# Coarser picks, later listing and a re-planned order in a two-layer PEER backbone

## The chip, the cores and the metric

One core of one Trainium2 chip runs the whole program. The metric is device microseconds of one execution. Engines are named as in the profile: PE (matrix products) with PEld (its weight loads), DVE (vector), ACT (scalar), POOL, and SP, which issues most loads.

## What is computed

The reference is a backbone of two layers over 256 tokens of width 1024. Layer 0 mixes state-space (SSD) and latent-attention heads (`hybrid`), layer 1 is a chunked gated MLP (`gmlp`). Each layer has modulation vectors (`cond @ ada_w`) and ends in a PEER block: each token picks, in each of 8 heads, its 16 best of 128 x 128 experts by two keys, and adds them, gated.

```python
q = (t @ wq).reshape(n_tok, PEER_HEADS, PEER_DKEY)
s1 = einsum('thd,hkd->thk', q[..., :half], k1); s2 = einsum('thd,hkd->thk', q[..., half:], k2)
v1, i1 = top_k(s1, 16); v2, i2 = top_k(s2, 16)
top_s, j = top_k(v1[..., :, None] + v2[..., None, :], 16)      # flattened 16 x 16
idx = 128 * i1 + i2 at j;  gate = softmax(top_s)
act = gelu(einsum('phkd,pd->phk', u_tab[idx], t))
out = einsum('phk,phkd->pd', gate * act, v_tab[idx])
```

## The kernel before

All engines run in-order queues. Their order is set while the program is built, by a planner: `Clock` keeps a modelled time for each engine, `Engine.cost` gives each instruction a price, and `schedule()` always takes the next step of whichever generator (a stream of work) is ready soonest. A `yield` of a condition, such as `at(tile)`, holds a stream back until the modelled clock says that the tile is there. So prices in `cost` move instructions, though they change nothing on the chip. Every recorded instruction goes through one wrapper, and thus stands at line L169 in the profile (L173 in the changed kernel).

**The modulation products** (`ada_group`) load 128 x 512 pieces of `ada_w` into a few buffers `aw` and multiply each by `condT` into 32 of 128 rows of a PSUM tile. They are strewn among the other products of `hybrid`, at the planner's choice.

**The PEER block** (`peer`) treats the experts by their first index, the class. The 75 classes 0 to X-1 are done densely: 75 S tiles (`products`, `pa<-phf,wr`) score 128 experts each for all 256 tokens, 75 V tiles (`pb<-wr,ge`) multiply the weighted scores by the value table. Tile data come through four buffers `wr`, loaded from SP's queue. Between them stands `spread`: 32 blocks of 8 tokens whose gates DVE writes out as one-hot tables (`o`, `oc`); PE multiplies these (`pb<-oc,o`), and DVE, or ACT where the score is not there yet, applies the result to `ge`. No V tile may begin before the last block is applied (the flag "G").

The experts of the other 53 classes are gathered. Each of two token tiles has CAP = 56 own rows: for row s, POOL fetches for each of 128 tokens one expert's u and v (2,048 floats, 1.05 MB a row) by an indirect DMA (`rows<-in_uv,gidx`), DVE takes the dot product (`junk`), ACT the GELU and gate, and DVE adds the weighted v (`acc`). Six row buffers (NR) are in use, and a row's `acc` comes two rows (LAG) after its dot. What does not fit into 56 goes to three shared rows: `listing` counts the leftovers of each token (`cnt`), sums them with small matrix products, builds `cmp` and `spot`, and PE adds the shared rows into the V sums (`pb<-rows,sc`).

Which experts a row holds comes from the picks. `choose` builds a key per expert and token, (row, place) packed into one float, and `take8` picks the 8 largest: one MAX8, one MATCH_REPLACE, small operations, and eight 128-wide `mk` operations that look up the gates. Nine picks per token tile are made, two of them ahead of the spread (EARLY), the rest one by one inside `gather`, between rows; only after the last does `listing` start. `ending` stores the sum of the first token tile (`acs`) and loads it again through SP's queue, in order with the tile loads.

Of the kernel before, what the change touches and what calls it, by code (L numbers as in the profile page):

```python
# [28 lines left out]
ROOM = 36  # L29
TB, TL = 8, 4  # L30
CAP = 56
ROUNDS = 9
# [18 lines left out]
KORDER = (8, 10, 12, 0, 2, 4, 6, 14)  # L51
LAG = 2
# [78 lines left out]
class Engine:  # L131
# [5 lines left out]
    def __getattr__(self, op):  # L137
        f = getattr(self.eng, op)

        def call(*args, **kw):  # L140
# [5 lines left out]
            if op == "indirect_dma_start":  # L146
# [3 lines left out]
                self.clock.run("D", 0.06 + 1.4e-3 * outs[0].shape[1], outs, ins, 2.0)  # L150
# [22 lines left out]
    def cost(self, op, outs, ins):  # L173
        aps = outs + ins
        if self.name == "T":
            n = 1
            for x in aps[-1 if op == "matmul" else 0].shape[1:]:
                n *= x
            return max(0.025, n * (0.00167 if aps[1].dtype == F32 else 0.00042)) * (0.25 if aps[0].shape[0] == 32 else 1.0)
        n = 1  # L180
        for x in aps:
            m = 1
            for y in x.shape[1:]:
                m *= y
            n = max(n, m)
        if self.name == "S":
            return (0.24 if len(ins) > 2 else 0.1) + 0.00083 * n
        if self.name == "G":
            return 0.1 + 0.00215 * n
        if all(x.dtype == F16 for x in aps):  # L190
            return 0.07 + n * 0.00052
        if op == "tensor_scalar":
            return 0.18 + n * 0.00105 if ins[0].tensor.name[:3] in ("pa_", "pb_") else 0.12 + n * 0.00054
        return (0.12 if op == "scalar_tensor_tensor" else 0.06) + n * 0.00105
# [3 lines left out]
def tile_backbone(ctx: ExitStack, tc: tile.TileContext, a: dict, out: bass.AP):  # L198
# [51 lines left out]
    def mm(o, lhsT, rhs, start=True, stop=True):  # L250
        T.matmul(o, lhsT, rhs, start=start, stop=stop)
# [50 lines left out]
    LEFT = 8 * ROUNDS - CAP  # L302
# [191 lines left out]
    def ada_group(l, g, get, bufs, ps):  # L494
# [3 lines left out]
        for i in range(len(units) + n - 1):  # L498
            if i < len(units):
                k, t = units[i]  # L500
                aw = bufs[i % n]
                yield lambda: clk["T"] >= clock.idle(aw)
                Q.dma_start(out=aw, in_=a["ada_w"][l, k * P:(k + 1) * P, g * 2048 + t * 512:g * 2048 + (t + 1) * 512])
            if i >= n - 1:
                k, t = units[i - n + 1]
                aw = bufs[(i - n + 1) % n]
                yield at(aw)
                mm(ps[32 * t:32 * t + 32, :], condT[:, k, :], aw, k == 0, k == KD - 1)
# [904 lines left out]
    def peer(l, mod, a2, sh2):  # L1413
# [4 lines left out]
        key = [[q1.tile([P, P], F32, name=f"key{t}{i}") for i in range(2)] for t in range(2)]  # L1418
        iota_i = key[0][0].bitcast(I32)
        G.iota(iota_i, [[1, P]], base=0, channel_multiplier=0)  # L1420
        jp1 = q1.tile([P, P], F32, name="jp1")
        V.tensor_scalar(jp1, iota_i, 1.0, None, op0=ALU.add)
# [16 lines left out]
        gidx = [q1.tile([P, 8 * ROUNDS], I32, name=f"gidx{t}") for t in range(2)]  # L1439
        gsel = [q1.tile([P, 8 * ROUNDS], F32, name=f"gsel{t}") for t in range(2)]  # L1440
# [48 lines left out]
        def stage2(t):  # L1489
# [94 lines left out]
            V.scalar_tensor_tensor(key[t][0], cg, 256.0, jp1, op0=ALU.mult, op1=ALU.add)  # L1584
            V.tensor_tensor(key[t][0], key[t][0], mk, op=ALU.mult)
            pks.append(pk)
# [3 lines left out]
        EARLY = 2  # L1590
# [7 lines left out]
        def take8(t, r_, idx=None, gsl=None):  # L1598

            if idx is None:  # L1600
                idx, gsl = gidx[t][:, 8 * r_:8 * r_ + 8], gsel[t][:, 8 * r_:8 * r_ + 8]
            ks = q2.tile([P, 8], F32, tag="ks", name="ks")
            V.max(ks, key[t][r_ % 2])
            V.match_replace(key[t][(r_ + 1) % 2], ks, key[t][r_ % 2], 0.0)
            ki = q2.tile([P, 8], I32, tag="ki", name="ki")
            V.tensor_copy(ki, ks)
            z_ = q2.tile([P, 8], F32, tag="z_", name="z_")
            V.tensor_scalar(z_, ks, 0.0, 65536.0, op0=ALU.is_equal, op1=ALU.mult)
            V.tensor_scalar(idx, ki, 8, None, op0=ALU.logical_shift_right)
            V.tensor_tensor(idx, idx, z_, op=ALU.add)  # L1610
            V.tensor_scalar(ki, ki, 255, None, op0=ALU.bitwise_and)
            j1 = q2.tile([P, 8], F32, tag="j1", name="j1")
            V.tensor_copy(j1, ki)
# [146 lines left out]
        def choose():  # L1760
# [8 lines left out]
            for r_ in range(EARLY):  # L1769
                take8(0, r_)  # L1770
# [38 lines left out]
        def listing():  # L1809

            ps = pa()
            rhs = q2.tile([P, 2, 2], F32, tag="rhs", name="rhs", bufs=1)
            V.memset(rhs, 1.0)
            for t in range(2):
# [9 lines left out]
                V.tensor_reduce(fl, key[t][ROUNDS % 2], axis=AX.X, op=ALU.max)  # L1824
                V.tensor_scalar(fl, fl, 0.0, None, op0=ALU.is_gt)
                mm(ps[:, t:t + 1], tri, cnt[:, t:t + 1], True, t == 0)
# [3 lines left out]
                mm(ps[:, 3 + 2 * t:4 + 2 * t], ones, fl)  # L1830
# [3 lines left out]
            V.tensor_tensor(ends[:, 2:4], ends[:, 2:4], ps[:, 4:6], op=ALU.add)  # L1834
            ps = pa()
            for k in range(SHARED):
                for t in range(2):
                    cmp = q2.tile([P, P], F32, tag="cmp", name="cmp", bufs=4)
                    V.tensor_scalar(cmp, iotaL[:, :P], float(k * P), ends[:, t:t + 1], op0=ALU.add, op1=ALU.is_ge)
# [291 lines left out]
```

## Time and profile before

| what | value |
| --- | --- |
| time, median of 3 runs | 2041.65 us (2041.55 to 2047.14) |
| the profiled execution | 2042.83 us, of which the span 2041.0 us |
| PE busy | 1886.9 us, 92% of the span |
| DVE busy | 1429.6 us, 70% |
| POOL, ACT busy | 630.8 us, 545.9 us |
| mean granted clock of PE | 0.961 |
| V products begin | 841.11 us (first layer), 1716.72 us (second) |

Busy time is an average over stages: PE is nearly always busy, so the time can only shrink where PE stands idle or where its own work shrinks. The idle places are read from the waits and from the timeline, stage by stage: the hybrid mix up to some 400 us, the stretch of scores and spread, the V products, and the end of each layer.

### The profile page before, as it was taken

What the parts mean: (1) busy time and instruction counts of PE and PEld (TensorE: products, weight loads), DVE (VectorE), ACT (ScalarE), POOL (GpSimd) and SP (SyncE); (2) the same over time, 40 slices, a digit from 0 to 9 for tenths busy, and PEclk for the clock granted to TensorE, in tenths of its full rate; (3) what the DMA queues carried; (4) which work ended last, traced back from release to release, by engine and by line L of the source; (5) the groups of instructions that cost most, each with busy time, mean ns of one, the idle gap of its engine ahead of it and who ended that gap; (6) DMA issues with size and microseconds to landing.
All of it is one profiled execution on the core that took longest, in us unless ns stands there. A gap on an engine that the chain in (4) does not pass through costs nothing.

```text
span 2041.0 us, 28033 instructions
## 1 busy us (share of the span) xinstructions
PE 1886.9 (92%) x9728; PEld 1516.0 (74%) x9728; DVE 1429.6 (70%) x3796; ACT 545.9 (27%) x1438; POOL 630.8 (31%) x402
## 2 busy tenths in 40 slices
PE   7899999999989999987999798999899999978997
PEld 3666444479968888876878588789778888867785
DVE  3565576246996888879767526478988888697665
ACT  4434253354212222110111254443122221101111
POOL 2324312176011112232422279551112112224221
PEclk9999999999989999999899899999989999988999
DMA  8555664545366889998899464453578888988993
GB/s 298 181 172 200 225 222 138 190 160 187 129 225 241 286 306 336 351 377 313 316 417 394 175 227 164 140 192 127 188 295 294 325 324 319 366 316 318 417 402 132
DMA packets 133065, 529.87 MB, mean 260 GB/s; under 512 B 17941, under 2 KB 18133, under 8 KB 105197
## 3 DMA queue, kind: packets, MB, share of 16 engines
q1 hardware_dynamic: 97440, 301.76, 41.8%
q0 software_dynamic: 34176, 225.07, 29.1%
q8 instruction: 77, 1.26, 0.3%
q10 hardware_dynamic: 1296, 1.16, 0.2%
q14 instruction: 76, 0.62, 0.1%
HBM read 540.28 MB, written 6.91 MB: 268 GB/s over the span
## 4 chain that ended last, share of the span: by engine, by line
PE 36%; issue 29%; DVE 17%; POOL 12%; ACT 2%; DMA 2%; POOLq 0%; SPq 0%; ACTq 0%; DVEq 0%
PE pa L169 23%; PE pb L169 14%; POOL rows L169 10%; DVE ge L169 6%; POOL whl L169 2%; DVE rows L169 1%; DVE acc L169 1%; DMA rows<-hs,lidx 1%; DVE oc L169 1%; DVE junk L169 1%; DVE mk L169 1%; DVE x L169 1%; DVE o L169 1%; DVE cacc L169 0%; POOLq L169 0%
## 5 line engine op out<-in xcount | busy, mean ns | idle before, releaser
L169 POOL DMA_INDIRECT rows<-in_uv,gidx x224 | 266.8, 1191 | 930.0 <-DVE acc L169 619.9
L169 PE MATMUL pb<-wr,ge 128*128 128x256 f32 x2400 | 542.1, 386 | 13.1 <-DMA wr<-in_dn 11.3
L169 PE MATMUL pa<-phf,wr 128*128 128x256 f32 x2400 | 539.8, 385 | 0.0
L169 PEld LDWEIGHTS pb<-wr,ge 128*128 128x128 f32 x2400 | 458.5, 193 | 96.5 <-DMA wr<-in_dn 32.1
L169 PEld LDWEIGHTS pa<-phf,wr 128*128 128x128 f32 x2400 | 459.8, 193 | 62.0
L169 POOL TENSOR_TENSOR whl<-wr,whl 128x1024 fp32r<-128x1024 f32 (+2 forms) x130 | 314.7, 2434 | 363.6 <-ACT whl L169 337.4
L169 DVE SCALAR_TENSOR_TENSOR junk<-rows,h 128x1024 bf16<-128x1024 f32 x224 | 273.5, 1221 | 99.9 <-DMA rows<-in_uv,gidx 99.7
L169 DVE SCALAR_TENSOR_TENSOR acc<-rows,wt,acc 128x1024 f32<-128x1024 f32 x220 | 281.8, 1281 | 0.0
L169 ACT ACTIVATE act<-act 128x1 f32<-128x1 f32 x230 | 47.0, 204 | 547.3 <-DVE junk L169 531.8
L169 ACT CAST whl<-wr 128x1024 fp32r<-128x1024 f32 (+2 forms) x136 | 136.9, 1019 | 74.5 <-issue 26.4
L169 ACT ACTIVATE sg<-pa 128x256 f32<-128x256 f32 (+25 forms) x116 | 34.4, 296 | 352.4 <-PE pa L169 313.1
L169 PE MATMUL pb<-oc,o 128*128 128x75 f16 x1024 | 85.3, 252 | 28.6 <-DVE oc L169 26.8
L169 PEld LDWEIGHTS <-o 128*128 128x128 f16 x1024 | 78.2, 118 | 38.0 <-DVE o L169 16.5
L169 PE MATMUL pa<-phh,whl 128*128 128x256 f32 x512 | 96.3, 285 | 2.6 <-DVE phf L169 2.2
L169 PE MATMUL pb<-aw,condT 128*32 128x512 f32 x328 | 94.0, 624 | 3.5 <-DVE mod L169 2.7
L169 DVE SCALAR_TENSOR_TENSOR ge<-pb,ge 128x80 f32<-128x80 f32 (+31 forms) x128 | 37.0, 323 | 73.4 <-ACT ge L169 73.2
L169 PEld LDWEIGHTS pa<-phh,whl 128*128 128x128 f32 x512 | 80.8, 191 | 4.7 <-DVE phf L169 2.5
L169 DVE SCALAR_TENSOR_TENSOR mk<-jp,j,gte 128x128 f32<-128x128 f32 x288 | 81.5, 348 | 1.3
L169 PE MATMUL pa<-phl,whl 128*128 128x256 f32 x256 | 73.2, 286 | 2.3 <-POOL phl L169 1.3
L169 ACT ACTIVATE wt<-act,gsel 128x1 f32<-128x1 f32 x224 | 66.0, 295 | 7.3
L169 PE MATMUL pb<-whl,cath 128*128 128x512 f32 x192 | 61.8, 400 | 2.0 <-POOL whl L169 1.2
L169 ACT ACTIVATE ge<-pa 128x256 f32<-128x256 f32 (+24 forms) x136 | 40.2, 296 | 81.4 <-PE pa L169 81.4
(525 smaller groups left out, 2436.2 us busy)
## 6 DMA issues: line engine op xcount, KB each, us to landing
wr<-in_dn SPq DMA_DIRECT2D x300, 512.0 KB, 6.6
aw<-in_ada_w SPq DMA_DIRECT2D x164, 256.0 KB, 3.3
wr<-in_wq SPq DMA_DIRECT2D x32, 512.0 KB, 3.2
wr<-in_w_out SPq DMA_DIRECT2D x16, 512.0 KB, 3.3
wr<-in_gm_w_v SPq DMA_DIRECT2D x16, 512.0 KB, 3.6
wr<-in_gm_w_u SPq DMA_DIRECT2D x16, 512.0 KB, 3.4
wr<-in_gm_w_out SPq DMA_DIRECT2D x16, 512.0 KB, 3.2
wr<-in_w_xbc SPq DMA_DIRECT2D x12, 512.0 KB, 4.8
```

The costliest lines, as they stand in the source:

```text
L169: return f(*args, **kw)
```

## The change

Seven things are changed. (1) The planner's prices are replaced by others, so that the order of every engine changes. (2) Picks are taken 24 at a time (three per token tile, one of them early); two further keys carry the gate in two parts, so that the eight `mk` operations go; keys are replaced in place. (3) `listing` yields four steps before its first products and three before its second; all `cmp` tiles are made first. (4) `mm` splits an fp32 product of 512 columns and 128 output rows into two of 256. (5) `ada_group` loads and multiplies two pieces at a time. (6) A shared row's product waits LATE = 6.0 longer on the modelled clock. (7) ROOM, a limit on SBUF, is 38 instead of 36.

```diff
-ROOM = 36
+GHI, GLO = 65535.0, 32767.0
+ROWS = 8192
+ROOM = 38
-ROUNDS = 9
+TAKE, TAKES = 24, 3
+LATE = 6.0
...
-            return max(0.025, n * (0.00167 if aps[1].dtype == F32 else 0.00042)) * (0.25 if aps[0].shape[0] == 32 else 1.0)
+            if aps[0].shape[0] == 32:
+                return 0.45
+            return max(0.06, n * (0.00168 if aps[1].dtype == F32 else 0.00046 if aps[1].dtype == F32R else 0.00095))
...
     def mm(o, lhsT, rhs, start=True, stop=True):
+        if rhs.dtype == F32 and lhsT.dtype == F32 and len(rhs.shape) == 2 and rhs.shape[1] == 512 and o.shape[0] == P:
+            T.matmul(o[:, :256], lhsT, rhs[:, :256], start=start, stop=False)
+            T.matmul(o[:, 256:], lhsT, rhs[:, 256:], start=False, stop=stop)
+            return
...
-        for i in range(len(units) + n - 1):
+        for i in range(0, len(units) + n, 2):
+            if i >= n:
+                yield at(*bufs[i % n:i % n + 2])
+                for j in range(2):
+                    k, t = units[i - n + j]
+                    mm(ps[32 * t:32 * t + 32, :], condT[:, k, :], bufs[i % n + j], k == 0, k == KD - 1)
...
-            V.scalar_tensor_tensor(key[t][0], cg, 256.0, jp1, op0=ALU.mult, op1=ALU.add)
+            V.scalar_tensor_tensor(key[t][0], jd, float(ROWS), cg, op0=ALU.mult, op1=ALU.add)
             V.tensor_tensor(key[t][0], key[t][0], mk, op=ALU.mult)
+            V.tensor_scalar(gi, gte[t], GHI, None, op0=ALU.mult)
+            V.scalar_tensor_tensor(cg, gte[t], GHI, gi, op0=ALU.mult, op1=ALU.subtract)
+            V.scalar_tensor_tensor(key[t][1], jd, 65536.0, gi, op0=ALU.mult, op1=ALU.add)
+            V.tensor_scalar(gi, cg, GLO, 32768.0, op0=ALU.mult, op1=ALU.add)
+            V.scalar_tensor_tensor(key[t][2], jd, 65536.0, gi, op0=ALU.mult, op1=ALU.add)
+            for i in (1, 2):
+                V.tensor_tensor(key[t][i], key[t][i], mk, op=ALU.mult)
-        EARLY = 2
+        EARLY = 1
...
-            V.max(ks, key[t][r_ % 2])
-            V.match_replace(key[t][(r_ + 1) % 2], ks, key[t][r_ % 2], 0.0)
+            for e in range(0, TAKE, 8):
+                for i in range(3):
+                    V.max(ks[i][:, e:e + 8], key[t][i])
+                for i in range(3):
+                    V.match_replace(key[t][i], ks[i][:, e:e + 8], key[t][i], 0.0)
...
-            for s_ in range(8):
-                mk = q2.tile([P, P], F32, tag="mk", name="mk")
-                V.scalar_tensor_tensor(mk, jp1, j1[:, s_:s_ + 1], gte[t], op0=ALU.is_equal, op1=ALU.mult, accum_out=gsl[:, s_:s_ + 1])
+            V.tensor_scalar(lo, kc, 1.0 / (GLO * GHI), -32768.0 / (GLO * GHI), op0=ALU.mult, op1=ALU.add)
+            V.scalar_tensor_tensor(gsl, kb, 1.0 / GHI, lo, op0=ALU.mult, op1=ALU.add)
+            V.tensor_tensor(gsl, gsl, ok, op=ALU.mult)
...
-                    if s % 8 == 0 and s // 8 >= taken[t]:
-                        take8(t, taken[t])
+                    if s % TAKE == 0 and s // TAKE >= taken[t]:
+                        take(t, taken[t])
...
         def listing():
+            for _ in range(4):
+                yield
+            ps = pa()
...
+            for _ in range(3):
+                yield
             ps = pa()
...
                     if pend[0][0] == 2:
-                        yield at(pend[0][3])
+                        yield lambda: clk["T"] >= clock.ready(pend[0][3]) + LATE
```

How the order moves is shown at three places of PE's queue. The first is the first layer, from an S tile (eight products of 256 columns, shown as rows that end in x and a count) to the first block of the spread (`o`, `oc`). Before:

```order
L169 MATMUL pa<-phf,wr 128x256 x80
...
L169 MATMUL pa<-phf,wr 128x256 x56
...
L169 MATMUL pa<-phf,wr 128x256 x32
L169 LDWEIGHTS o_4524
L169 MATMUL pb<-oc,o_4524 128x75
```

And changed:

```order
L173 MATMUL pa<-phf,wr 128x256 x128
...
L173 MATMUL pa<-phf,wr 128x256 x80
...
L173 MATMUL pa<-phf,wr 128x256 x32
L173 LDWEIGHTS o_4673
L173 MATMUL pb<-oc,o_4673 128x75
```

In the three stretches, between which transposes stand, 168 products or 21 S tiles come ahead of the first block before, 240 or 30 now, in either layer; the last block now stands behind S tile 75 (behind 69 and 73 before).

The second place is the end of the first layer on PE: the products of `listing` (`cnt`, `fl`, `cmp`), the V tiles, and the shared rows (`rows`, `sc`). Before:

```order
L169 MATMUL pb<-wr,ge 128x256 x120
L169 MATMUL pa<-cnt,tri 128x1
...
L169 MATMUL pb<-wr,ge 128x256 x8
L169 MATMUL pa<-rhs,cmp 128x2 x6
L169 MATMUL pb<-wr,ge 128x256 x320
L169 MATMUL pb<-rows_4515,sc 128x512 x4
L169 MATMUL pb<-rows_4511,sc 128x512 x4
L169 MATMUL pb<-rows_4513,sc 128x512 x4
L169 MATMUL pb<-wr,ge 128x256 x24
```

And changed:

```order
L173 MATMUL pb<-wr,ge 128x256 x104
L173 MATMUL pa<-cnt,tri 128x1
...
L173 MATMUL pb<-wr,ge 128x256 x24
L173 MATMUL pa<-rhs,cmp 128x2 x6
L173 MATMUL pb<-wr,ge 128x256 x336
L173 MATMUL pb<-rows_4664,sc 128x256 x8
L173 MATMUL pb<-rows_4660,sc 128x256 x8
L173 MATMUL pb<-rows_4662,sc 128x256 x8
```

The shared rows moved behind all V tiles (72 of 75 stood ahead of them before, 71 in the second layer), and three V tiles instead of one lie between the two groups of `listing`. On DVE `cnt` moved from behind row 70 to behind row 63.

The third place is the hybrid mix on PE, where the modulation products (`aw`) stand between others. Before:

```order
L169 MATMUL pb<-aw_323,condT 32x512
L169 MATMUL pa<-ident,xch 128x128 x4
L169 MATMUL pb<-aw_324,condT 32x512
L169 MATMUL pb<-whl,hh 128x384 x2
...
L169 MATMUL pb<-aw_325,condT 32x512
L169 MATMUL pb<-aw_326,condT 32x512
```

And changed:

```order
L173 MATMUL pa<-aw_310,condT 32x512
L173 MATMUL pa<-aw_311,condT 32x512
L173 MATMUL pa<-ident,cum 32x128 x2
L173 MATMUL pa<-aw_312,condT 32x512
L173 MATMUL pa<-aw_313,condT 32x512
L173 MATMUL pb<-ident,xch 128x128 x8
```

They now come in twos at least. In the whole program the 164 products stand in 82 runs before (27 single, 39 of two, 5 of three, 11 of four) and in 57 now (one single, 30 of two, one of three, 25 of four). Products that fill PE's idle time at the start (warm-up) go from 58 to 34.

## Rows read from the trace of the kernel before

**Rows 1.** The page: busy time, instructions; a group (busy us, mean ns | idle before).
```profile
PE 1886.9 (92%) x9728; PEld 1516.0 (74%) x9728; DVE 1429.6 (70%) x3796; ACT 545.9 (27%) x1438; POOL 630.8 (31%) x402
...
L169 DVE SCALAR_TENSOR_TENSOR ge<-pb,ge 128x80 f32<-128x80 f32 (+31 forms) x128 | 37.0, 323 | 73.4 <-ACT ge L169 73.2
```

**Rows 2.** Who waited for whom, whole span, PE: us in total, times, longest us.
```profile
PE pa L169 <- DVE cnt L169: 28.0, 2, 14.3
PE pb L169 <- DVE oc L169: 26.8, 11, 8.8
```

**Rows 3.** Timeline of PE, score products and first spread block, either layer: start us, us.
```profile
582.39 14.05 PE L169 MATMUL pa<-phf,wr 128*128 128x256 f32 x64
605.03 1.63 PE L169 MATMUL pb<-oc,o 128*128 128x75 f16 x16 [8.59 <-DVE oc L169]
...
655.34 2.63 PE L169 MATMUL pb<-oc,o 128*128 128x75 f16 x32
...
1479.11 0.23 PE L169 MATMUL pb<-oc,o 128*128 128x75 f16 x1 [8.82 <-DVE oc L169]
```

**Rows 4.** Timeline of PE, where the V products of either layer begin.
```profile
841.11 55.51 PE L169 MATMUL pb<-wr,ge 128*128 128x256 f32 x256
...
1716.72 62.56 PE L169 MATMUL pb<-wr,ge 128*128 128x256 f32 x288
```

**Rows 5.** Timeline of DVE: two successive rows where nothing is picked.
```profile
1033.74 1.23 DVE L169 SCALAR_TENSOR_TENSOR junk<-rows,h 128x1024 bf16<-128x1024 f32 x1 [1.34 <-DMA rows<-in_uv,gidx]
...
1037.52 1.22 DVE L169 SCALAR_TENSOR_TENSOR junk<-rows,h 128x1024 bf16<-128x1024 f32 x1 [1.35 <-DMA rows<-in_uv,gidx]
```

**Rows 6.** Windows of 50 us: busy us by engine (instructions), granted clock, DMA share, GB/s.
```profile
900.00:950.00 50.00, 42.93 (x190) 37.14 (x189) 41.13 (x188) 3.98 (x16) 12.35 (x8) 0.93 0.94 360
950.00:1000.00 50.00, 36.31 (x163) 31.73 (x162) 40.29 (x148) 4.48 (x18) 18.23 (x12) 0.83 0.77 262
1000.00:1050.00 50.00, 49.69 (x224) 41.66 (x223) 33.50 (x43) 6.47 (x26) 15.33 (x14) 1.00 1.02 418
1800.00:1850.00 50.00, 34.17 (x159) 30.35 (x157) 48.38 (x220) 3.97 (x16) 13.83 (x9) 0.81 0.79 272
```

**Rows 7.** Timeline, all engines, end of the first layer.
```profile
1127.57 1.22 DVE L169 SCALAR_TENSOR_TENSOR junk<-rows,h 128x1024 bf16<-128x1024 f32 x1
...
1145.80 0.41 DVE L169 TENSOR_SCALAR sc<-iotaL,spot,wt 128x256 f32<-128x256 f32 x1 [0.60 <-ACT wt L169]
...
1149.80 10.52 PE L169 MATMUL pb<-wr,ge 128*128 128x256 f32 x48
```

**Rows 8.** Timeline, all engines, end of the second layer.
```profile
1994.55 1.23 DVE L169 SCALAR_TENSOR_TENSOR junk<-rows,h 128x1024 bf16<-128x1024 f32 x1
...
2013.02 0.41 DVE L169 TENSOR_SCALAR sc<-iotaL,spot,wt 128x256 f32<-128x256 f32 x1 [0.60 <-ACT wt L169]
...
2017.02 13.98 PE L169 MATMUL pb<-wr,ge 128*128 128x256 f32 x64
```

**Rows 9.** Timeline of PE: modulation products (aw), four together and one alone.
```profile
162.04 1.07 PE L169 MATMUL pb<-aw,condT 128*32 128x512 f32 x8
...
165.89 1.04 PE L169 MATMUL pb<-aw,condT 128*32 128x512 f32 x2
```

**Rows 10.** Timeline of PE: two 512-column fp32 products of the attention scores.
```profile
341.88 1.12 PE L169 MATMUL pb<-krT,qr 64*128 64x512 f32 x2
342.94 1.13 PE L169 MATMUL pa<-kn,qn 128*128 128x512 f32 x2
```

**Rows 11.** Timeline of DVE, first layer: one pick of eight between two rows.
```profile
929.08 0.29 DVE L169 MAX8 ks<-key 128x8 f32<-128x128 f32 x1
...
932.91 1.28 DVE L169 SCALAR_TENSOR_TENSOR acc<-rows,wt,acc 128x1024 f32<-128x1024 f32 x1
```

**Rows 12.** Row dots (DVE) before the V products: first, then second layer.
```profile
L169 DVE SCALAR_TENSOR_TENSOR junk<-rows,h x41: 1212/1218/1222, 609.0 to 838.6; 128x1024 bf16<-128x1024 f32 x41
...
L169 DVE SCALAR_TENSOR_TENSOR junk<-rows,h x44: 1211/1218/1244, 1483.1 to 1714.4; 128x1024 bf16<-128x1024 f32 x44
```

More of the change, by code (lines that the diff above doesn't have):

```diff
@@ L497, in ada_group @@
         n = len(bufs)
-        for i in range(len(units) + n - 1):
-            if i < len(units):
[L500 to L508, printed above, removed]
+        for i in range(0, len(units) + n, 2):
[4 more added lines that the diff above has]
+                    mm(ps[32 * t:32 * t + 32, :], condT[:, k, :], bufs[i % n + j], k == 0, k == KD - 1)
+            if i < len(units):
+                yield lambda: clk["T"] >= max(clock.idle(x) for x in bufs[i % n:i % n + 2])
+                for j in range(2):
+                    k, t = units[i + j]
+                    Q.dma_start(out=bufs[i % n + j], in_=a["ada_w"][l, k * P:(k + 1) * P, g * 2048 + t * 512:g * 2048 + (t + 1) * 512])
         ada_tail(get(), ps)
@@ L1416, in peer @@
         q2 = es.enter_context(tc.tile_pool(name="q2", bufs=2))
-        key = [[q1.tile([P, P], F32, name=f"key{t}{i}") for i in range(2)] for t in range(2)]
+        key = [[q1.tile([P, P], F32, name=f"key{t}{i}") for i in range(3)] for t in range(2)]
         iota_i = key[0][0].bitcast(I32)
         G.iota(iota_i, [[1, P]], base=0, channel_multiplier=0)
-        jp1 = q1.tile([P, P], F32, name="jp1")
-        V.tensor_scalar(jp1, iota_i, 1.0, None, op0=ALU.add)
+        jd = q1.tile([P, P], F32, name="jd")
+        V.tensor_scalar(jd, iota_i, -1.0, float(P), op0=ALU.mult, op1=ALU.add)
         place_i = q1.tile([P, SHARED], I32, name="place_i")
@@ L1438, in peer @@
         pkT = [q1.tile([P, 4, P], F16, name=f"pkT{t}") for t in range(2)]
-        gidx = [q1.tile([P, 8 * ROUNDS], I32, name=f"gidx{t}") for t in range(2)]
-        gsel = [q1.tile([P, 8 * ROUNDS], F32, name=f"gsel{t}") for t in range(2)]
+        gidx = [q1.tile([P, TAKE * TAKES], I32, name=f"gidx{t}") for t in range(2)]
+        gsel = [q1.tile([P, TAKE * TAKES], F32, name=f"gsel{t}") for t in range(2)]
         gte = [q1.tile([P, P], F32, name=f"gte{t}") for t in range(2)]
@@ new lines, in take @@
+                idx, gsl = (x[t][:, TAKE * r_:TAKE * (r_ + 1)] for x in (gidx, gsel))
+            tmp = lambda n, dt: q2.tile([P, TAKE], dt, tag=n, name=n)
+            ks = [tmp(f"ks{i}", F32) for i in range(3)]
+            for e in range(0, TAKE, 8):
[3 more added lines that the diff above has]
+                    V.match_replace(key[t][i], ks[i][:, e:e + 8], key[t][i], 0.0)
+            ki, kb, kc = (tmp(f"k{n}", I32) for n in "ibc")
@@ L1769, in choose @@
             for r_ in range(EARLY):
-                take8(0, r_)
+                take(0, r_)
                 yield
@@ L1823, in listing @@
                 fl = q2.tile([P, 1], F32, tag="fl", name="fl")
-                V.tensor_reduce(fl, key[t][ROUNDS % 2], axis=AX.X, op=ALU.max)
+                V.tensor_reduce(fl, key[t][0], axis=AX.X, op=ALU.max)
                 V.tensor_scalar(fl, fl, 0.0, None, op0=ALU.is_gt)
+                fls.append(fl)
+            for _ in range(4):
+                yield
+            ps = pa()
+            for t in range(2):
                 mm(ps[:, t:t + 1], tri, cnt[:, t:t + 1], True, t == 0)
@@ L1834, in listing @@
             V.tensor_tensor(ends[:, 2:4], ends[:, 2:4], ps[:, 4:6], op=ALU.add)
+            cmps = []
+            for k in range(SHARED):
+                for t in range(2):
+                    cmp = q2.tile([P, P], F32, tag="cmp", name="cmp", bufs=2 * SHARED)
+                    V.tensor_scalar(cmp, iotaL[:, :P], float(k * P), ends[:, t:t + 1], op0=ALU.add, op1=ALU.is_ge)
+                    cmps.append(cmp)
+            for _ in range(3):
+                yield
             ps = pa()
@@ L1837, in listing @@
                 for t in range(2):
-                    cmp = q2.tile([P, P], F32, tag="cmp", name="cmp", bufs=4)
-                    V.tensor_scalar(cmp, iotaL[:, :P], float(k * P), ends[:, t:t + 1], op0=ALU.add, op1=ALU.is_ge)
-                    mm(ps[:, 2 * k:2 * k + 2], cmp, rhs[:, t, :], t == 0, t == 1)
+                    mm(ps[:, 2 * k:2 * k + 2], cmps[2 * k + t], rhs[:, t, :], t == 0, t == 1)
             yield
```

70 lines of the change are left out of this document (37 added, 33 removed).

## The prediction

> **What bounds the kernel now.** I read the page first: PE is busy for 1886.9 of 2041.0 us [rows 1], so at most 154 us of its idle time can be won, and beyond that only PE's own work. The list of waits then says where PE stands: 28.0 us in two waits for `cnt`, one in each layer, and 26.8 us for `oc`, the one-hot tables of the spread [rows 2]. The timeline shows the places.
>
> *Scores and spread.* Four S tiles, 64 instructions, take 14.05 us, so a tile takes 3.5 [rows 3]. In the first layer PE stands 8.59 us before its first spread block at 605.03, so it came there at 596.4; in the second 8.82 before 1479.11, at 1470.3 [rows 3]. 54 S tiles (187.4 at 3.47, which is 55.51 us over 16 tiles of the same products [rows 4]) and 32 blocks at about 1.3 (2.63 for two [rows 3]) are then to come, 229 us; without a stall the V products would begin at 825.4 and 1699.3. They begin at 841.11 and 1716.72 [rows 4]: 15.7 and 17.4 us are lost to DVE.
>
> *V products.* Here the gather sets the pace. Where nothing is picked, rows come 3.77 us apart, and each waits 1.3 us for its transfer [rows 5]; that window's DMA share is 1.02, at 418 GB/s [rows 6]. Where eight are picked between two rows, the share falls to .94, .77 and (second layer) .79, and PE's clock to between .81 and .93 [rows 6]: there DVE is the bound. PE ends by waiting for `cnt`, which needs all picks.
>
> *Ends.* The last own row's dot starts at 1127.57, the third `sc` ends at 1146.2, and then PE still has four products of that row and 10.52 us of V tiles, until 1160.3 [rows 7]. In the second layer: 1994.55, 2013.4, and 13.98 us of V tiles until 2031.0 [rows 8].
>
> **The change, part by part.** The sum is made against 2042.83 us, the profiled execution, 1.2 above the median of the runs.
>
> *Modulation products.* Four together take 1.07 us and one alone 1.04 [rows 9], since each fills 32 of 128 rows. What counts is runs: 82 become 57, 25 x 1.05 = 26 us of PE's time. PE is near full in this stage, but it has idle gaps that new loads can fall into: I take 18, bounds 0 and 26. Loads are made two at a time, so each first piece waits for its neighbour; SP's queue holds the same 164 loads, and the planner places the products behind them.
>
> *Halves.* In the attention scores 512-column fp32 products start 1.06 us apart [rows 10]; two products of 256 take 2 x .434 = .87 (55.51 over 128 products) [rows 4]. 32 such products give 6 at most; most stand between waits for other engines. I take 2, bounds 0 and 6. The Trainium skill ("TensorE: Matmul & The Clock Gate", section "Back-to-back issue gap") has a matmul's spacing grow with its columns plus a small fixed term, so that two halves pay that term twice; by it this term is 0 and the forecast 2 us higher. Hybrid mix in all: **-20**, bounds 0 and -32.
>
> *Spread, first layer.* The first block moves from S tile 21 to 30, so PE works 31 us more before it needs `oc`, which covers the stall of 8.6 and the key building that is added: eight 128 x 128 operations per token tile, 16 x .3 (a MAX8 of that size took .29 [rows 11]) = 4.8 on DVE. Up to the V products DVE dots 41 rows [rows 12]; by DVE's order 39 stand ahead of the last block now, which itself is the last thing before V: two rows less, at 1.22 and 1.28 us for `junk` and `acc` [rows 5, 11], -5. The early pick of 24 costs about what the two of 8 did. Four later picks of 3.8 (929.08 to 932.91 [rows 11]) become one of 24. Such a pick is 9 MAX8 and 9 MATCH_REPLACE at .29, 5.2, and 12 narrow operations for which no row stands alone: between nothing and .2 each, and I take 7.5 (the dear end, because they follow one another). So DVE saves 5 + 15.2 - 7.5 - 4.8 = 8, and would be done at 833; PE could at 825.4. I take 832: **-9**, bounds 0 and -15.7. The two rows come later: **+5**, up to 7.5 at the row pace.
>
> *V products, first layer.* Twelve picks follow after V's start before (12 x 3.8 = 46 us of DVE), four now (30). That is 16, bounded by the transfers' slack: (.06 + .23) x 50 = 14.5 us in the two windows [rows 6]. `listing` follows, with `cnt` seven rows earlier and its `cmp` ready before PE asks, so PE's 14 us goes with it and isn't counted again: **-14**, bounds 0 and -14.5.
>
> *End, first layer.* Shared rows behind all V tiles: the end is then the third `sc`, 18.6 us after the last dot, and 8 halves, 3.5 us, 22.1 in place of 32.8 [rows 7]. I take **-10**. The V tiles fill what was idle. `acs` is stored three tiles later on SP's queue and read back right behind it, which holds tile loads there; four tile buffers cover 4 x 3.47 = 13.9 us [rows 4], so nothing. POOL issues the same gathers in the same order; the leftovers' fetches come behind row 72 instead of later, nothing.
>
> First layer: -9 + 5 - 14 - 10 = **-28**. The second by the same steps: V starts at 1701 (-16, where PE is the limit, since DVE has 8 rows less, 44 to 36 [rows 12]), those rows come later (+20, up to 30), picks -14, end 36.4 to 22.4, taken as -12: **-22**.
>
> Sum: 2042.8 - 20 - 28 - 22 = **1973 us**.
>
> **Rivals.**
>
> *Transfers are the bound throughout the V products.* Then picks were hidden, and rows left over cost what an earlier V start gives. For it: the DMA share of 1.02 and the wait of 1.3 us per row [rows 5, 6]. Against: the shares of .77 and .79 where picks are [rows 6]. Left are the ends, 22, and half of the hybrid's 20: 2042.8 - 32 = **2011**. The Trainium skill ("DMA: Bandwidth & Descriptors", section "Where 436 GB/s comes from") names about 358 GB/s as what HBM gives one core; the 418 GB/s of this trace lies above. By the page a row and a tile, 1.57 MB, would take 4.4 us, not 3.77.
>
> *PE is the bound throughout.* Both stalls of the spread (33), the waits for `cnt` (28), the ends (22) and all 32 of the hybrid go, and the rows left over hide behind PE: 2042.8 - 115 = **1928**. For it: PE at 92%. Against: the transfers' share of 1.02.
>
> *DVE sets the spread, and it starts later: slower.* DVE's queue is in order: it stands at the first block's result, with rows and tables behind it, until PE brings that block, now at 596.4 + 31.2 = 627.6. If the stretch from there to V keeps its length, 236.1 us, less the 8 saved, V begins at 856, 15 late; in the second layer no earlier than now. That alone leaves 2013. But the page has 73.4 us in which DVE waits for ACT's `ge` before applying a block [rows 1], 37 a layer, and 32 blocks now fall among 45 S tiles, not among 48 to 52. Where that wait doubles, V begins 52 late and 37 late: first layer +52 + 5 - 14 - 10 = +33, second +37 + 20 - 14 - 12 = +31, hybrid -20, in all **2087**. It decides for slower from 15 us more per layer on. Against it: PE has more tiles scored ahead, so that more of `ge` is there.
>
> *The change does not do what it says.* Pairs of loads come late and return what runs save, and an order made with other prices opens as many gaps as it shuts: **about 2040**.
>
> **How the numbers follow.** The forecast has .60, the transfers .20, PE alone .08, DVE .07, nothing .05. A difference under 0.3%, 6 us, can't be told from none. Faster: .60 + .20 + .08 = .88; same .05; slower .07. The range runs from 1940 to 2020: below, the hybrid's full 32, V at PE's limit, and a part of the rows left over hidden; above, the transfers' 2011 and what its ends may fail to give. It leaves out PE alone, DVE and nothing, .20 together.
>
> **What would show it.** Right: first spread block without a stall, V near 832 and 1690 to 1700; windows after V's start at a DMA share near 1 and a clock near 1; no wait for `cnt`; about 22 us from the last own dot to the end of PE's sums; `aw` busy near 68 instead of 94. Wrong: V later than 841 with DVE waiting for ACT's `ge`; last own dots as late after V's start as now; the `aw` products waiting for their loads.

## The result and the profile after

The changed kernel takes 1990.59 us (median of 4 runs, 1982.73 to 1996.46), against 2041.6 of the kernel before in the same comparison: 0.9743 of its time, 95% interval 0.9704 to 0.9783, or 51 us less. The forecast was 1973, the range 1940 to 2020. The profiled execution took 1996.46 us, so the stages below are some 6 us long in all. This kernel's runs differ by 14 us among themselves, and stages of two executions by 2 to 5.

The page of the changed kernel, the answer to [rows 1]. Its second line is the applying of the spread's blocks, before which DVE waits 56.5 us for ACT's `ge`, where it was 73.2.

```profile
PE 1863.6 (93%) x9888; PEld 1539.0 (77%) x9888; DVE 1369.0 (69%) x3376; ACT 540.2 (27%) x1428; POOL 629.5 (32%) x400
...
L173 DVE SCALAR_TENSOR_TENSOR ge<-pb,ge 128x292 f32<-128x292 f32 (+19 forms) x128 | 42.1, 370 | 59.4 <-ACT ge L173 56.5
```

PE's busy time fell by 23, DVE's by 61. PE's list of waits shows what went and what came (us in total, times, longest):

```profile
PE pb L173 <- DVE sc L173: 19.1, 2, 10.9
PE pb L173 <- DMA wr<-in_dn: 17.5, 4, 9.9
PE pb L173 <- DVE oc L173: 13.6, 5, 4.0
```

The two waits for `cnt` of 14 us [rows 2] are gone. The wait for `oc` is half of its 26.8. That for tiles (`wr`) is 17.5; it was 11.3 in the kernel before.

The first spread block, on PE and then on DVE, is the answer to [rows 3]. By PE's timeline, PE comes to it behind S tile 30 and doesn't wait:

```profile
599.62 14.03 PE L173 MATMUL pa<-phf,wr 128*128 128x256 f32 x64
613.49 2.48 PE L173 MATMUL pb<-oc,o 128*128 128x75 f16 x32
...
619.30 1.32 PE L173 MATMUL pb<-oc,o 128*128 128x75 f16 x16
```

DVE's timeline at the same place:

```profile
594.86 0.85 DVE L173 TENSOR_TENSOR oc<-eq,pkT 128x600 f16<-128x600 f16 x2
...
596.75 0.85 DVE L173 TENSOR_TENSOR oc<-eq,pkT 128x600 f16<-128x600 f16 x2
614.84 0.69 DVE L173 TENSOR_TENSOR o<-iotaJ,pkT 128x1024 f16<-128x1024 f16 x1 [17.24 <-PE pb L173]
```

But DVE had the tables `oc` of the first two blocks at 595.7 and 597.6. It has two buffers for them, and the third table, at the head of its queue, stood 17.24 us until PE had read the first. Rows that lay behind it in the queue lay still too.

V products begin at 822.97 and 1669.10, and 39 and 36 rows are dotted by then, the answers to [rows 4] and [rows 12]. PE's timeline in the first layer:

```profile
822.97 59.19 PE L173 MATMUL pb<-wr,ge 128*128 128x256 f32 x272
```

The dots up to there, first layer (name and count, ns of one, first and last start):

```profile
L173 DVE SCALAR_TENSOR_TENSOR junk<-rows,h x39: 1215/1218/1224, 616.7 to 797.2; 128x1024 bf16<-128x1024 f32 x39
```

And in the second layer:

```profile
L173 DVE SCALAR_TENSOR_TENSOR junk<-rows,h x36: 1216/1219/1227, 1468.0 to 1627.3; 128x1024 bf16<-128x1024 f32 x36
```

After V's start, windows of 50 us (columns as in [rows 6]) show the share of the transfers at .93 to 1.02 and PE's clock at .86 or more, the picks among them:

```profile
900.00:950.00 50.00, 44.22 (x211) 38.67 (x210) 42.09 (x136) 4.97 (x20) 16.82 (x11) 0.93 0.97 368
950.00:1000.00 50.00, 49.85 (x229) 42.94 (x228) 30.31 (x46) 6.46 (x26) 19.38 (x15) 1.00 1.00 398
1000.00:1050.00 50.00, 49.59 (x215) 39.52 (x214) 32.20 (x40) 6.47 (x26) 12.99 (x14) 1.00 1.02 416
1750.00:1800.00 50.00, 40.06 (x180) 34.64 (x179) 40.36 (x135) 5.31 (x22) 15.10 (x10) 0.86 0.93 357
```

And the ends, the answers to [rows 7, 8]. After the last own dot comes the first `sc`, and then nothing but the shared rows' products, 48 instructions; the timeline of all engines, first layer:

```profile
1102.86 1.22 DVE L173 SCALAR_TENSOR_TENSOR junk<-rows,h 128x1024 bf16<-128x1024 f32 x1
...
1109.84 13.36 PE L173 MATMUL pb<-rows,sc 128*128 128x256 f32 x48 [8.22 <-DVE sc L173]
```

The same view of the second layer's end:

```profile
1960.06 1.22 DVE L173 SCALAR_TENSOR_TENSOR junk<-rows,h 128x1024 bf16<-128x1024 f32 x1
...
1967.18 12.70 PE L173 MATMUL pb<-rows,sc 128*128 128x256 f32 x48 [10.91 <-DVE sc L173]
...
1980.41 0.69 DVE L173 TENSOR_TENSOR x<-pb,ge 128x512 f32<-128x512 f32 x1 [4.27 <-DMA rows<-hs,lidx]
```

From such rows the time is laid out by stage. "Sums ready" is DVE's first read of a finished V sum (`x<-pb,ge`): at 1156.05 and 2026.72 before, 1123.83 and 1980.41 after.

| stage, us | before | after | difference | forecast |
| --- | --- | --- | --- | --- |
| start to the first S tile | 522.3 | 509.3 | -13.0 | -20 |
| first layer: S tiles and spread | 318.8 | 313.7 | -5.1 | -9 |
| V's start to the last own dot | 286.5 | 279.9 | -6.6 | -9 (+5 - 14) |
| to sums ready | 28.5 | 20.9 | -7.6 | -10 |
| gated MLP, to the second layer's first S tile | 240.1 | 236.8 | -3.3 | none |
| second layer: S tiles and spread | 320.6 | 308.5 | -12.1 | -16 |
| V's start to the last own dot | 277.8 | 291.0 | +13.2 | +6 (+20 - 14) |
| to sums ready | 32.2 | 20.3 | -11.9 | -12 |
| rest | 14.3 | 14.3 | 0 | 0 |

The sum is -46.4, and -70 was forecast. The stages of the forecast are there, all with its sign; what is missing lies in the hybrid mix, in the spread, and in the second layer after V's start.

### The profile page after: what moved, and what is told of

Same layout as the page of the kernel before. It is cut to its first block, busy times and chain, and to the rows that moved or that the text cites. A ratio compares the mean times of both kernels' runs of the same rounds, so it can differ in the third digit from the quotient of the medians.

```text
span 1994.7 us, 27972 instructions
## 1 busy us (share of the span) xinstructions
PE 1863.6 (93%) x9888; PEld 1539.0 (77%) x9888; DVE 1369.0 (69%) x3376; ACT 540.2 (27%) x1428; POOL 629.5 (32%) x400
## 5 line engine op out<-in xcount | busy, mean ns | idle before, releaser
L173 PE MATMUL pb<-wr,ge 128*128 128x256 f32 x2400 | 539.5, 384 | 19.5 <-DMA wr<-in_dn 17.5
L173 PEld LDWEIGHTS pb<-wr,ge 128*128 128x128 f32 x2400 | 453.7, 191 | 103.1 <-DMA wr<-in_dn 41.9
L173 POOL TENSOR_TENSOR whl<-wr,whl 128x1024 fp32r<-128x1024 f32 (+2 forms) x128 | 310.6, 2440 | 306.6 <-ACT whl L173 298.9
L173 ACT ACTIVATE sg<-pa 128x8 f32<-128x8 f32 (+20 forms) x98 | 26.5, 270 | 278.1 <-PE pa L173 252.3
L173 PE MATMUL pb<-oc,o 128*128 128x75 f16 x1024 | 85.3, 252 | 14.8 <-DVE oc L173 13.6
L173 ACT ACTIVATE ge<-pa 128x256 f32<-128x256 f32 (+18 forms) x146 | 46.9, 321 | 144.9 <-PE pa L173 144.3
L173 PE MATMUL pa<-aw,condT 128*32 128x512 f32 x320 | 78.7, 605 | 6.9 <-DMA aw<-in_ada_w 5.1
L173 DVE SCALAR_TENSOR_TENSOR ge<-pb,ge 128x292 f32<-128x292 f32 (+19 forms) x128 | 42.1, 370 | 59.4 <-ACT ge L173 56.5
L173 PE MATMUL pa<-phl,whl 128*128 128x256 f32 x256 | 73.2, 286 | 2.4 <-POOL phl L173 1.3
L173 DVE TENSOR_TENSOR o<-iotaJ,pkT 128x1024 f16<-128x1024 f16 x64 | 43.8, 684 | 36.8 <-PE pb L173 36.8
L173 DVE MAX8 ge<-ge 128x8 f32<-128x128 f32 (+1 forms) x192 | 38.4, 254 | 26.0 <-ACT ge L173 25.9
```

The source lines that it names most:

```text
L173: return f(*args, **kw)
```

## Experiments

All times are medians of five or six runs, in four groups; the kernel before took 2041.7, 2043.0, 2044.3 and 2040.7 us in them. The groups were made to tell which part carried the gain, and what became of the missing 18 us.

### The changed kernel again

No edit.

> The changed kernel again, as the yardstick of this group. Both theories: 1983 to 1996 us, about 0.974 of before.

Measured: 1989.07 us, 0.9730 of before (0.9703 to 0.9757). This is the yardstick; its stages agree with the table above to 3 us.

### Without the detour of acs

In the changed kernel SP's queue stands twice in each layer. The rows of its queue in the first layer are these (issues; the second column is the time over which a group was issued):

```profile
882.20 5.05 SPq L173 DMA_DIRECT2D wr<-in_dn  x2
893.97 0.33 SPq L173 DMA_DIRECT2D acs<-acc  x1
894.39 3.21 SPq L173 DMA_DIRECT2D wr<-in_dn  x3
903.31 0.33 SPq L173 DMA_DIRECT2D ge<-acs  x1
903.74 8.47 SPq L173 DMA_DIRECT2D wr<-in_dn  x2
```

And PE's timeline there, with its wait for a tile:

```profile
906.48 29.55 PE L173 MATMUL pb<-wr,ge 128*128 128x256 f32 x128 [5.78 <-DMA wr<-in_dn]
```

The store waits for the last `acc` of the first token tile, and the load of the same data waits until the store has landed, with tile loads behind it; PE then waits 5.78 us for a tile, and in the second layer 9.94. DVE waits 6.9 us for the store as well, since the second token tile sums into the same place. The edit gives each token tile a place of its own, the second the one in `ge` that V tiles have left:

```diff
-        acc = [spare[0], q1.tile([P, D], F32, name="acc")]
+        acc = [q1.tile([P, D], F32, name="acc"), spare[0]]
...
-                if t == 0 and s == CAP - 1:
-                    Q.dma_start(out=acs, in_=acc[1])
...
+                    if pend[0][:2] == (1, 0):
+                        while "held" not in done:
+                            yield lambda: "held" in done
                     accumulate()
...
-                if t == 0:
-                    Q.dma_start(out=acc[0], in_=acs)
```

> The changed kernel, but the first token tile's sum stays where it is and the second sums into its own place, so that the store and the load of acs go. Theory 1 (SP's queue holds tile loads behind that store and load, and DVE waits for the store): PE's waits for wr of 5.8 and 9.9 us and DVE's of 6.9 and 6.7 us go, 12 to 16 us less than the changed kernel, about 1977. Theory 2 (transfers alone set the pace after the V products begin): only the bytes go, 2.1 MB at 418 GB/s, 5 us less, about 1986.

Measured: 1979.1 us, 0.9690 (0.9657 to 0.9724), 10 less than the yardstick in the medians, between the two theories; the intervals overlap a little. In PE's list of waits those for `wr` fell to 8.1 us from 16.4 in the yardstick:

```profile
PE pb L173 <- DVE oc L173: 13.5, 5, 4.0
...
PE pb L173 <- DMA wr<-in_dn: 8.1, 4, 4.7
```

From V's start to the last dot it is 277.3 and 282.5 us, against 280.8 and 289.0: 10 us. That is less than PE's waits and DVE's together, since the transfers went on through most of the hold: their share between 900 and 950 is .97.

### Picks of 24 alone

The kernel before with `take`, the three keys and EARLY = 1. Of the rest of the change two small things are in it as well: ROOM = 38, and all `cmp` tiles made first.

```diff
-        def take8(t, r_, idx=None, gsl=None):
+        def take(t, r_, idx=None, gsl=None):
...
+            for e in range(0, TAKE, 8):
+                for i in range(3):
+                    V.max(ks[i][:, e:e + 8], key[t][i])
```

> The kernel before with nothing but the picks of 24 by three keys (old prices, single aw, 512-column products, old listing, no LATE). Theory 1 (picks cost what they keep the transfers from, 18 us over both layers): from V's start to the last own dot some 9 us less in each layer, waits for cnt under 10 us, 2020 to 2025. Theory 2 (the new prices' order makes the gain, picks were hidden behind transfers): within 6 us of before.

Measured: 2010.36 us, 0.9837 (0.9811 to 0.9863), 31 less than before: more than theory 1 gave, and far from theory 2. From V's start to the last own dot it takes 264.1 and 259.2 us, 41 less than before in both layers. Part of that is rows: 45 are dotted ahead of V in each layer, where it had been 41 and 44. The ends are 12 us longer over both layers. In PE's list of waits, `cnt` still has 17.9 of its 28.0; theory 1 had under 10.

```profile
PE pb L173 <- DVE oc L173: 24.5, 13, 7.6
PE pa L173 <- DVE cnt L173: 17.9, 2, 9.7
```

### Old prices in the changed kernel, and new prices in the kernel before

```diff
-            if aps[0].shape[0] == 32:
-                return 0.45
-            return max(0.06, n * (0.00168 if aps[1].dtype == F32 else 0.00046 if aps[1].dtype == F32R else 0.00095))
+            return max(0.025, n * (0.00167 if aps[1].dtype == F32 else 0.00042)) * (0.25 if aps[0].shape[0] == 32 else 1.0)
```

and so for all of `cost` and the transfers' price; the second kernel has the same edit the other way, on the kernel before.

> The changed kernel with the planner's old prices. Theory 1 (picks, shared rows' place and aw in pairs make most of it): 1995 to 2008, of the 51 us no more than 17 given back, those of the spread. Theory 2 (prices make the gain): 2020 or more.

> The kernel before with nothing but the planner's new prices (picks of 8, single aw, whole products, old listing). Theory 1 (prices gain in the hybrid mix and lose as much in the PEER blocks, where the first block comes behind S tile 30 and DVE stands before it): 2030 to 2042, with DVE waiting 10 us or more for PE before each layer's third table. Theory 2 (prices and picks each make about half of the gain): 2010 to 2020.

Measured: 1993.41 us with old prices, 0.9748 (0.9719 to 0.9776), and 2015.32 for new prices alone, 0.9860 (0.9840 to 0.9879). Taken out of the changed kernel, the prices cost 4 us, within the spread of its runs and just below what theory 1 had. Put alone on the kernel before they gain 28. DVE's wait before tables, 20.6 us in the first layer of that kernel, is as theory 1 had it, but the total is theory 2's. So neither theory holds whole: prices alone do make about half, but the rest of the change makes nearly all of it without them. In the kernel with new prices alone, this is the wait for tables in DVE's list of waits:

```profile
DVE o L169 <- PE pb L169: 41.3, 3, 20.6
```

By stage the reason shows:

| stage, us | before | new prices alone | old prices in the changed kernel | changed (again) |
| --- | --- | --- | --- | --- |
| start to the first S tile | 522.3 | 507.7 | 514.2 | 507.0 |
| S tiles and spread, two layers | 639.4 | 655.5 | 635.2 | 620.7 |
| V's start to the last own dot, two layers | 564.3 | 556.0 | 522.8 | 569.8 |
| to sums ready, two layers | 60.7 | 40.1 | 66.7 | 40.3 |
| rows dotted before V | 41, 44 | 45, 45 | 45, 45 | 39, 36 |

New prices shorten the hybrid mix by 15 us (by 7 in the changed kernel) and the ends by 20 to 26, with the shared rows behind all V tiles. In the changed kernel they also shorten the spread by 15, but leave 15 rows more to the stage after V's start, which then takes 47 us longer. That stage takes the prices' gain. On the kernel before it is the other way round: 45 rows are dotted ahead of V in each layer, and the spread takes 16 us longer.

### One modulation product at a time, whole products, LATE = 0

Each is one edit to the changed kernel: `ada_group` as before; `mm` without the halves; and

```diff
-LATE = 6.0
+LATE = 0.0
```

> The changed kernel with the modulation products loaded and multiplied one at a time, as before. Theory 1 (each run of aw products costs PE a time of its own): the first S tile starts 8 to 12 us later than 507, total 1997 to 2001. Theory 2 (the products fill gaps anyway): within 4 us of the changed kernel.

> The changed kernel without the halves: 512-column fp32 products whole. Theory 1 (columns alone set the time of a product): the attention scores' products busy as long either way, 35 to 36 us, total within 4 us of the changed kernel. Theory 2 (a whole product costs .2 more than two halves): 6 us longer, 4 of them before the first S tile.

> The changed kernel with LATE = 0, so that the shared rows' products may stand earlier among the V tiles. Theory 1 (their place makes the shorter ends, 8 and 12 us): PE waits for sc with V tiles still behind, 15 to 20 us longer, about 2007. Theory 2 (earlier picks alone bring the ends forward): within 4 us.

Measured: 1992.62 us (0.9757, 0.9742 to 0.9771), 1986.77 (0.9728, 0.9709 to 0.9748) and 1983.66 (0.9730, 0.9687 to 0.9773). None differs from the yardstick by more than the runs do.

Single `aw` products: with the new prices the planner put them together anyway, into 59 runs where the pairs make 57, and the first S tile starts at 507.8. So what theory 1 would show isn't shown, since the runs didn't come apart. PE's groups of all these products (busy us, mean ns | idle before) say something of what runs are worth; first the kernel with picks alone, which has the old prices and the old `ada_group`:

```profile
L173 PE MATMUL pb<-aw,condT 128*32 128x512 f32 x328 | 96.3, 629 | 3.1 <-DVE mod L173 2.5 <-DMA aw<-in_ada_w 0.6
```

Then the changed kernel with single products:

```profile
L173 PE MATMUL pa<-aw,condT 128*32 128x512 f32 x320 | 83.7, 613 | 10.3 <-DMA aw<-in_ada_w 5.3 <-DVE mod L173 5.0
L173 PE MATMUL pb<-aw,condT 128*32 128x512 f32 x8 | 2.9, 601 | 0.0
```

In the kernel before it was 94.0, in 82 runs; in the changed kernel 81.6, in 57 (78.7 and 2.9 in two groups). With single products it is 86.6, in 59 runs; with old prices and pairs 81.6, in 69. So the count of runs doesn't set it. The products that stand alone go with it better: the kernel before has 27 of them, the one with single products ten, the other two one each.

Whole products: PE's groups of 18 of the 32 attention scores' products, whole,

```profile
L173 PE MATMUL pa<-krT,qr 64*128 64x512 f32 x18 | 10.1, 641 | 0.0
L173 PE MATMUL pa<-kn,qn 128*128 128x512 f32 x18 | 9.9, 630 | 0.0
```

and in halves, in the kernel without LATE,

```profile
L173 PE MATMUL pa<-krT,qr 64*128 64x256 f32 x36 | 10.1, 402 | 0.0
L173 PE MATMUL pa<-kn,qn 128*128 128x256 f32 x36 | 9.9, 398 | 0.0
```

give 20.0 us for 18 products (two instructions each) whole, and 20.0 for the same 18 in halves, 1.11 a product either way. Theory 1 holds for these products: their columns alone count.

LATE = 0: the shared rows' products stand behind all 75 V tiles without it too, so their place comes from the prices, not from LATE (with old prices and LATE = 6.0 they stand behind 70). Theory 1 falls, with 5 us less in place of 15 to 20 more; that earlier picks alone moved the ends is not shown by it (picks alone left them at 36 us in each layer, new prices alone brought them to 20).

### Lower prices for DVE

DVE's rows show where its price came from. These are some of the operations of one pick of 24, and what follows it:

```profile
907.52 0.68 DVE L173 MAX8 ks<-key 128x8 f32<-128x128 f32 x3
...
908.17 0.28 DVE L173 MATCH_REPLACE8 key<-ks,key 128x128 f32<-128x128 f32 x1
...
908.43 0.28 DVE L173 MATCH_REPLACE8 key<-ks,key 128x128 f32<-128x128 f32 x1
...
911.61 0.17 DVE L173 CAST ki<-ks 128x24 int32<-128x24 f32 x1
911.68 0.17 DVE L173 CAST kb<-ks 128x24 int32<-128x24 f32 x1
...
913.14 1.28 DVE L173 SCALAR_TENSOR_TENSOR acc<-rows,wt,acc 128x1024 f32<-128x1024 f32 x1
```

A MAX8 alone takes .29 [rows 11], and three in a row take .68, so they start .2 apart. A MATCH_REPLACE of .28 has the next .26 after it, and operations on 24 columns, .17 long, start .07 apart. Instructions overlap, and the new prices are whole durations (.28 for a MAX8): the planner thinks DVE later than it is, and puts the first block behind S tile 30. That the prices are the reason for tile 30 is a guess, which the next kernels try. The edit lowers DVE's fixed prices by .06 on top of the kernel without the detour, then by .02 and .08, and by .06 with the detour:

```diff
-            return (0.24 if op == "match_replace" else 0.155) + 0.00097 * n
+            return (0.180 if op == "match_replace" else 0.095) + 0.00097 * n
...
-            return 0.155 + n * (0.00052 if wide else 0.00104)
+            return 0.095 + n * (0.00052 if wide else 0.00104)
```

> The kernel of e2 (no detour), with the planner's prices of DVE's instructions lowered by .06 each (the trace shows three MAX8 in .68 us, so they start .2 apart, priced at .28): the first spread block then stands behind S tile 26 rather than 30. Theory 1 (DVE's 17 us before the first block, in each layer, are rows left over for the transfer-bound stage, 2.5 us each): that wait under 4 us, 4 to 8 rows more before V, 10 to 20 us less than e2, about 1965. Theory 2 (rows dotted earlier only delay the spread): V starts later by as much, within 5 us of e2.

> The changed kernel, detour and all, with DVE's prices lowered by .06 as in e8. Theory 1 (where the first block stands is worth 30 to 38 us whatever else is done, and the detour 10): 1951 to 1959. Theory 2 (the hold of the detour takes most of it back, since rows and tiles come closer): 1965 or more.

> The kernel of e2 with DVE's prices lowered by .02 in place of .06: first block behind S tile 28, last behind 75. Theory 1 (DVE's wait before the first block is what was won): that wait about 10 us a layer, some 3 rows more than e2 before V, about 1960, halfway between e2 and e8. Theory 2 (the e8 gain comes from the order elsewhere, in the hybrid mix and the V products): no nearer to one than to the other, or as e2, 1979.

> The same lowered by .08: first block behind S tile 24, last behind 64. Theory 1: DVE waits for nothing before the first block, PE stands for its tables again (some 6 us a layer), the end of the spread leaves PE alone; 1945 to 1955. Theory 2: within 4 us of e8.

| kernel | us | of before | first S tile | rows before V | DVE waits for PE before a table | S tiles and spread, both layers | V's start to last dot, both layers | to sums ready, both layers |
| --- | --- | --- | --- | --- | --- | --- | --- | --- |
| no detour | 1979.1 | 0.9690 (0.9657 to 0.9724) | 505.6 | 39, 37 | 34.8 | 623.0 | 559.8 | 40.7 |
| lowered by .02 | 1988.24 | 0.9750 (0.9725 to 0.9775) | 517.3 | 34, 34 | 35.7 | 595.7 | 576.0 | 42.1 |
| lowered by .06 | 1941.21 | 0.9505 (0.9489 to 0.9522) | 499.1 | 44, 45 | 10.4 | 607.4 | 520.6 | 51.9 |
| lowered by .08 | 1944.93 | 0.9522 (0.9505 to 0.9539) | 517.3 | 45, 45 | none | 614.8 | 513.2 | 56.5 |
| .06 with the detour | 1942.98 | 0.9490 (0.9467 to 0.9512) | 505.2 | 44, 44 | 10.4 | 609.3 | 535.0 | 43.6 |

DVE's timeline before the third table in the first layer, at .06:

```profile
584.81 0.85 DVE L173 TENSOR_TENSOR oc<-eq,pkT 128x600 f16<-128x600 f16 x2
590.83 0.69 DVE L173 TENSOR_TENSOR o<-iotaJ,pkT 128x1024 f16<-128x1024 f16 x1 [5.17 <-PE pb L173]
```

The dots before V's start there:

```profile
L173 DVE SCALAR_TENSOR_TENSOR junk<-rows,h x44: 1215/1218/1222, 593.0 to 800.9; 128x1024 bf16<-128x1024 f32 x44
```

At .06 the time fell by 38 us, more than theory 1 had. DVE's wait fell to 5.2 a layer, 13 rows more came ahead of V, and the spread took 16 us less, where no gain was expected. V's stage took 39 us less and the ends 11 more: when the last own dot starts, PE still has V tiles to do (13.6 us of them in the first layer). How many rows come ahead of V shows in PE's waits for `sc`: 17.8 us without lower prices, none at .06 and .08, and at .02, with the fewest rows,

```profile
PE pb L173 <- DVE sc L173: 42.6, 4, 22.2
```

That DVE's wait before the third table left the rows over, as theory 1 has it, is not shown. Which rows stand ahead of the last block is fixed in DVE's queue when the program is built, and with new prices alone 41.3 us of the same wait go with 45 rows ahead in each layer. In the spread, moreover, DVE's wait for ACT's `ge` fell by 27 us (57.2 to 30.3), no less than the wait for tables (24). What either was worth alone was not tried, and the edit moves the rest of the order too: the hybrid mix is 6.5 us shorter.

At .08 the total is at the edge of theory 1's, 1945, and also within theory 2's 4 us of the kernel at .06, so it doesn't part them. DVE's wait is gone, and PE stands 7 us for `oc` in all (13.5 without lower prices, 4.1 at .06).

At .02 theory 1 failed: 1988, not 1960. The wait stayed (35.7), the rows ahead of V became fewer, not more, and the hybrid mix took 12 us longer. From the first S tile to sums ready, though, the two layers took 1213.8 us, 9.7 less than without lower prices: PE stood nowhere in the spread (busy for all of its 595.7 us). So time can be won there with the wait as it was. The step from the price to the place was wrong too: by the trace the first block stands behind S tile 29, not 28 (behind 26 at .06 and 24 at .08, as expected). The hybrid mix moves by up to 18 us between these orders (499.1 to 517.3); why is not settled.

With the detour the second theory was refuted, and the first one's range, 1951 to 1959, was missed as well: 1942.98, as low as without it. So the 10 us of the detour stand for the changed order only. In the profiled executions the stage after V's start is 14 us longer with it, with one row more to do there, and the ends are 8 us shorter; the medians show no difference.

The version lowered by .06 beats both kernels: 0.9505 of the kernel before, or 48 us less than the changed one.

## Why the prediction was right, and where it was off

**What bounds.** That DVE's picks kept the transfers from work after V's start was right, and shown by the kernel with picks alone: 31 us. The two waits for `cnt` did not go with them alone, as the sum had it: 17.9 of the 28.0 us stayed with picks alone, and with new prices alone, and picks of eight, there are none. The total alone doesn't tell the steps apart: the changed kernel with old prices, 1993.41, lies within the range as well, by quite other stages.

**Picks, -14 in each layer.** Right in size. In kernels with the detour and picks of 24, V's start to last dot takes 523.3 and 522.8 us where 90 rows are dotted ahead of V, and 569.8 where 75 are: 3.1 us a row. The kernel before had 85 ahead, for which that line gives 538, and it took 564.3: 26 us for the picks, an estimate. New prices alone, with picks of eight and 90 rows ahead, took 556.0, 33 more than the 523. Forecast were 28. A pick of 24 took 5.6 us (907.52 to 913.14), not the 7.5 that was taken; the transfers were the bound on the gain all the same.

**Rows left over, +5 and +20.** Their number was right to the row, 39 and 36, read from DVE's order. Their price was a little low: 2.5 us a row from DVE's own work, against 3.1 by the line above. In that line the kernel with 75 rows also has 16.4 us of PE's waits for tiles, the others 4.0 and less; without the detour (76 and 89 rows, 559.8 and 520.6) it is 3.0, and with detour and lower prices (88 rows, 535.0) 2.7. So ten rows cost 27 to 31 instead of 25.

**SP's queue, costed at nothing.** This term was wrong. "Four tile buffers cover 13.9 us" left out that the store itself waits for DVE (10.3 us at the longest in the list of SP's waits), and then the load for the store, two waits in a row on the same queue:

```profile
SPq L173 <- DVE acc L173: 17.5, 3, 10.3
```

The cover ran out, and PE waited 5.8 and 9.9 us (7.1 and 3.2 before). The kernel before has the detour as well, and its list of PE's waits had

```profile
PE pb L169 <- DMA wr<-in_dn: 11.3, 5, 7.1
```

So the change added some 5 us of such waits. The 10 us by which the stage is shorter without the detour, in the changed kernel's order, are the price of the whole detour.

**Spread, -9 and -16.** -5.1 and -12.1. The rise of the first block from tile 21 to 30 covered the stall of 8.6, as forecast. What the step didn't have is the other side: DVE stood 17 us in each layer for that late block. The third rival had this wait, with V delayed by it. With new prices alone V does come later: counted from the first S tile, 8.4 and 7.7 us later than in the kernel before, with 45 rows ahead of it. But DVE's wait for ACT's `ge` did not double, as that rival feared; it fell from 73.1 us to 32.4 there. In the changed kernel 10 rows fewer stand ahead of V, picks are shorter, and V is earlier. What the 17 us cost there alone no run shows. Lower prices took most of that wait away, half of the wait for `ge`, and changed the order of rows as well, for 38 us in all.

**Modulation products, -18.** Mis-sized. PE's time for them fell by 12.4 (94.0 to 81.6), not 26, and 1.05 for each run that goes is not the price: with old prices and pairs 69 runs take 81.6 too, with single products 59 take 86.6. What goes with it better is how many products stand alone, 27 before and one now; that was not tried by itself. The pairs were not even needed for the stage, whose first S tile new prices alone bring to 507.7. One sign of being wrong showed in small: PE waited 5.1 us for loads of `aw`, 0.7 before.

**Halves, -2.** Nothing, the bound that the rule in the Trainium skill gave ("TensorE: Matmul & The Clock Gate", section "Back-to-back issue gap"): 20.0 us for the same columns, whole or halved. Of the small fixed term per product that it adds, these rows show nothing. The .87 that was taken for two halves came from V tiles, and didn't carry over to these products: in halves they are busy as long as whole.

**Ends, -10 and -12.** -7.6 and -11.9, with the shared rows last. The reason was the order, as forecast, and it came from the prices: 20.2 and 19.9 with new prices alone, 35.2 and 31.5 in the changed kernel with old ones. LATE had no part in it.

**The rivals.** Transfers as the bound: half right, the stage runs at a share of .93 to 1.02 in the windows shown, and still gained from picks. Where the share is 1.02 it moves 416 GB/s, above the 358 that the Trainium skill names for one core ("DMA: Bandwidth & Descriptors", section "Where 436 GB/s comes from"), as in the kernel before; the measurement decides. PE alone: no; but at .06 lower prices PE is busy 95% of the span, and the kernel takes 1941. The gated MLP's 3 us were not forecast.

## What to carry to other kernels

When a block is moved later on one engine so that it needn't wait, look at the engine that makes its input: with two buffers it stands still from the third input on, and what lies behind it in its queue stands too. Count also the rows that an order leaves for a stage with little slack: here 2.7 to 3.1 us each. A planner's prices taken from recorded durations may be too high where instructions overlap: lowered by .06 us an instruction on DVE they gave an order that was 38 us faster, though which part of that order did it was not tried alone. Orders answer such prices by leaps (.02 won nothing), so several are to be timed. And parts of a change that reach the same gain by two ways (pairs and prices) are worth little when they are taken away one by one, so each should be tried alone on the kernel before as well.

## What was not expected of the hardware

Three MAX8 of 128 x 128 take .68 us in a row where one alone is recorded with .29, so successive DVE instructions overlap by some .09 us. An indirect row costs 2.7 to 3.1 us after V's start, by the stages of kernels that leave more or fewer of them; that is between its bytes at the measured 418 GB/s (2.5 us) and the pace of rows with a tile each (3.77 us).
